# Fetching the first token half's columns a block earlier, splitting block 7's sums, and ordering W2's splits last

## The chip, the cores and the metric

The kernel runs on one core of one Trainium2 chip. The metric is the device time of one execution in microseconds (us), as the median of several runs. TensorE is called PE here, VectorE DVE, ScalarE ACT, GpSimd POOL and SyncE SP. "L669" is line 669 of the kernel before.

## What is computed

One layer of a streaming encoder over 1024 tokens of 1024 channels, all in float32: a mixer (a convolution group and a retention group between one input and one output projection), then a feed-forward part, then a last norm.

```python
x = x + jnp.concatenate([a_out, b_out], axis=-1) @ w_out[l]
h = rms_norm(x, norm2_g[l])
x = x + jnp.square(jax.nn.relu(h @ w_ff1[l])) @ w_ff2[l]     # 1024 x 4096, 4096 x 1024
...
return rms_norm(x, final_g)
```

The change lies in the passage from the output projection to the feed-forward part, and at the seam between the feed-forward's two products.

## The kernel before

**Tiles.** Tokens are cut into 8 blocks of 128. Every float32 matmul is done as three matmuls of rounded halves (`mm3`, L137, with its lines 139 to 141): each operand is split into a high part, which ACT writes, and a low part, which DVE makes by subtraction. `split_evac` (L189, with lines 190 and 191) does this for a tile of 128 partitions.

**The feed-forward part as a 2 x 2 scheme with seven products.** W1's columns go in 16 pairs of 128-column blocks, tokens in two halves of 512 (blocks 0 to 3 and 4 to 7), channels in two halves. `strassen_pair` (L747) computes a pair with seven products of 512 columns, M1 to M7, each 4 steps of `mm3`, so 12 matmuls. M1 and M2 take the first token half's columns (B11, B21) and a plain W1 block. The other five need sums: of W1 blocks (`prep_sums`, L702, DVE lines 679 to 682, then splits), and of columns: T2 for M6, T1 for M5, T3 for M7, B22 for M3, T4 for M4. `prep_sums` loads two W1 blocks (L687) into a pool `rawp` of two buffers.

**Where the columns come from.** A block's output projection adds to the residual (L815). `normed_columns` (L619) then norms the block (L622), transposes it on PE (L632), and writes its columns. A block of the first half is split to B11 and B21, and a full copy goes to DRAM (L641, then L617 on ACT's queue). A block of the second half reads back the partner block's copies (L649 and L650, on SP's queue, 256 KB each in runs of 512 bytes), copies b12 (L652) and makes four sums (L653, L654, L657, L658) with their splits. T3 and T4 of blocks 4 to 6 go to DRAM (L617 on POOL's queue) and come back as one load each (L830, 768 KB, the "early" columns) to be split at L838; block 7's T3 and T4 are split at once.

**Order of the work.** The blocks run as ORDER = 0, 1, 4, 2, 5, 3, 6, 7, normed one block behind their projection. Four pairs (AHEAD = 4) are started before the second half is complete: a pair that runs ahead is a generator with stops after its first load and split, and after M1 and M2. The sequence behind the loop over blocks (L825 to L838): M1 and M2 of pair 0; new T3 and T4 tiles; the early columns' loads; block 7's columns and sums; M1 and M2 of pair 1; pairs 2 and 3; the splits of the early columns. Then each pair is run to its end, pair 0 first.

**What sets the order on an engine.** A list scheduler places instructions on each engine by the order in which they are written and by when it reckons their inputs ready. On the chip each engine and each queue then runs its list strictly in that order, waiting where an input is missing. Tiles come from pools with a fixed number of slots: `sp` has 11 of 2 KB per partition (sums, copies, fetched columns, hidden rows), `wp` 13 of 8 KB (columns and W2), `ps` and `pr` four PSUM banks each.

**The seam.** The second product (`ff2_group`, L864) loads W2 (L877) into `wp` slots that the last pair's column tiles give up, and the kept sums of the hidden rows (xr, L893); `split_unit` (L859) splits both. Its first product M1 adds into four banks of `ps`; one of these is the last pair's `pa`, read last by ACT rl (L728) and DVE hid (L723). `copy` (L758, ACT line 760) copies a product out of PSUM; PE may not add to that bank before.

Of the kernel before, what the change touches and what calls it, by code (L numbers as in the profile page):

```python
# [15 lines left out]
P = 128  # L16
# [25 lines left out]
def hybrid_layer_kernel(  # L42
# [89 lines left out]
    def load_split(src, scales):  # L132
        return split(load_raw(src), scales)

    pe_log, tap_log = [], []

    def mm3(acc, lh, ll, rh, rl, first, last, loose=False):  # L137
        kw = dict(skip_group_check=True) if loose else {}
# [47 lines left out]
                nc.tensor.transpose(out=pt[:, i], in_=src[:, d * P : (d + 1) * P], identity=ident)  # L186
            split_evac(pt, dst.quad(g, 0, t), dst.quad(g, 1, t))

    def split_evac(src, hi, lo):  # L189
        nc.scalar.activation(hi, src, AF.Copy)  # L190
        nc.vector.tensor_tensor(lo, src, hi.bitcast(F32), ALU.subtract)  # L191


# [421 lines left out]
    def keep_columns(name, cols, t):  # L615
        eng = nc.scalar if name in ("B11", "B21") else nc.gpsimd
        eng.dma_start(dram_cols[name][:, :, cols], t)  # L617

    def normed_columns(b, r):  # L619

        xn = cp.tile([P, D], F32, tag="c", name="xn")
        nc.vector.scalar_tensor_tensor(xn, flat(b), r, n2row, ALU.mult, ALU.mult)  # L622
        j, t = divmod(b, 4)
        cols = slice(t * P, (t + 1) * P)
        hl = lambda name: [h[:, :, cols] for h in hb[name]]
        new = lambda name: sp.tile([P, 4, P], F32, tag="s", name=name)
        pts = []
        for k in range(2):
            pt = pr.tile([P, 4, P], F32, tag="r", name="pt")
            for i in range(4):  # L630
                d = 4 * k + i
                nc.tensor.transpose(out=pt[:, i], in_=xn[:, d * P : (d + 1) * P], identity=ident)  # L632
            pts.append(pt)
        if j == 0:
            if t == 0:
                new_columns("B11")
                new_columns("B21")
            for name, pt in zip(("B11", "B21"), pts):
                split_evac(pt, *hl(name))
                full = new("full")  # L640
                nc.scalar.activation(full, pt, AF.Copy)  # L641
                keep_columns(name, cols, full)
            return
        if t == 0:
            new_columns("T2", True)
            new_columns("T1")
            new_columns("B22")
        b11, b21 = new("b11"), new("b21")
        nc.sync.dma_start(b11, dram_cols["B11"][:, :, cols])  # L649
        nc.sync.dma_start(b21, dram_cols["B21"][:, :, cols])  # L650
        b12, t2 = new("b12"), new("t2")
        nc.scalar.activation(b12, pts[0], AF.Copy)  # L652
        nc.vector.tensor_tensor(b11, b12, b11, ALU.subtract)  # L653
        nc.vector.tensor_tensor(t2, pts[1], b11, ALU.subtract)  # L654
        split_evac(t2, *hl("T2"))
        split_evac(b11, *hl("T1"))
        nc.vector.tensor_tensor(b12, pts[1], b12, ALU.subtract)  # L657
        nc.vector.tensor_tensor(b21, b21, t2, ALU.subtract)  # L658
        split_evac(pts[1], *hl("B22"))
        for name, full in (("T3", b12), ("T4", b21)):  # L660
            if b < NB - 1:
                keep_columns(name, cols, full)
            else:
                split_evac(full, *hl(name))

# [79 lines left out]
    def strassen_pair(p, ahead):  # L747

        a, b = {}, hb

        def product(acc, name, first, last):
            for d in range(4):
                mm3(
                    acc, a[name][0][:, d], a[name][1][:, d], b[name][0][:, d], b[name][1][:, d],
                    first and d == 0, last and d == 3, loose=True,
                )

        def copy(acc):  # L758
            t = sp.tile([P, HALF], F32, tag="s", name="part")
            nc.scalar.activation(t, acc, AF.Copy)  # L760
            return t

        def plus(acc, t):
            nc.vector.tensor_tensor(t, acc, t, ALU.add)
            return t

        raw = [load_w1(2 * p + i) for i in range(1 if ahead else 2)]
        split_named(a, raw[0], ("M1", "M2"))
        if ahead:
            yield  # L770
        if not ahead:
            prep_sums(a, raw)
        pa = ps.tile([P, HALF], F32, tag="mm", name="pa")
        product(pa, "M1", True, False)
        m1 = copy(pa)
        pb = pr.tile([P, HALF], F32, tag="r", name="pb")
        product(pb, "M2", True, True)
        c11 = square(plus(pb, m1))
        if p < NPAIR - 1:
            keep(p, "M1", c11)  # L780
        if ahead:
            yield
            prep_sums(a, [load_w1(2 * p + i) for i in range(2)])
            c11 = sp.tile([P, HALF], F32, tag="s", name="hid")
            nc.sync.dma_start(c11, xs[p]["M1"])
        product(pa, "M6", False, False)
        u2 = copy(pa)
        pb = pr.tile([P, HALF], F32, tag="r", name="pb")
        product(pb, "M5", True, False)
        m5 = copy(pb)  # L790
        product(pa, "M7", False, False)
        c22 = square(plus(pa, m5))
        product(pb, "M3", False, True)
        c12 = square(plus(pb, u2))
        product(pa, "M4", False, True)
        c21 = square(pa, relu(pa))
        if p < NPAIR - 1:
            keep_operands(p, c11, c12, c21, c22)
        else:
            for i, row in enumerate(((c11, c12), (c21, c22))):  # L800
                for j, t in enumerate(row):
                    nc.gpsimd.dma_start(last_hid[i][:, j * HALF : (j + 1) * HALF], t)
# [6 lines left out]
    for i, b in enumerate(ORDER):  # L809
        if i + 3 < NB:  # L810
            conv_norm(ORDER[i + 3])
        if i + 2 < NB:
            conv_side(ORDER[i + 2])
        for n, acc in enumerate(out_proj(woa, *sides.pop(b))):
            nc.vector.tensor_tensor(blk[b][:, n], acc, blk[b][:, n], ALU.add)  # L815
        m = tiny.tile([P, 1], F32, tag="nmr", name="m2")
        nc.gpsimd.tensor_tensor(m, mean_sq(flat(b)), eps1, ALU.add)
        rn[b] = tiny.tile([P, 1], F32, tag="r1", name="rn")
        nc.gpsimd.tensor_tensor(rn[b], m, mhalf[:, 0:1], ALU.pow)
        if i >= 6:  # L820
            next(pairs[i - 6])
        if i >= 1:
            normed_columns(ORDER[i - 1], rn.pop(ORDER[i - 1]))
    hb["M1"], hb["M2"] = hb["B11"], hb["B21"]
    next(pairs[0])  # L825
    for name in ("T3", "T4"):
        new_columns(name)
    early = slice(0, HALF - P)
    for name in ("T3", "T4"):
        nc.sync.dma_start(hb[name][1][:, :, early].bitcast(F32), dram_cols[name][:, :, early])  # L830
    normed_columns(NB - 1, rn.pop(NB - 1))
    next(pairs[1])
    for p in range(2, AHEAD):
        next(pairs[p])
        next(pairs[p])
    for name in ("T3", "T4"):
        hi, lo = (t[:, :, early] for t in hb[name])
        split_evac(lo.bitcast(F32), hi, lo)  # L838
    for product, name in (("M3", "B22"), ("M4", "T4"), ("M5", "T1"), ("M6", "T2"), ("M7", "T3")):
# [18 lines left out]

    def split_unit(src, n):  # L859
        w = wp.tile([P, 2, n, HALF], F32R, tag="w", name="w")  # L860
        split_evac(src, w[:, 0], w[:, 1])
        return w

    def ff2_group(group):  # L864
# [174 lines left out]
```

## Time and profile before

| | us |
|---|---|
| median of 3 runs | 1062.36 (1060.86 to 1062.65) |
| the profiled execution | 1062.97 |
| its span, first to last instruction | 1061.2 |
| PE busy in it | 1030.1 (97%) |
| DVE busy | 804.8 (76%) |
| ACT busy | 377.0 (36%) |
| POOL busy | 129.4 (12%) |

The profile is that of one execution; its times are counted from the first instruction. PE is busy for nearly all of the span, so its few idle stretches are looked at one by one: the timeline of an engine shows each instruction's start and length and, in brackets, the idle time before it and what ended that. A start on a queue (SPq, ACTq) is that of a transfer's issue; it lands later. The granted clock is the share of full speed that the throttle gives PE: 1.00 is 2.4 GHz, 0.50 is 1.2 GHz.

### The profile page before, as it was taken

The numbers are of one execution on the slowest core, as the hardware profiler recorded it, in microseconds if no ns is written. First come the engines' busy times: TensorE is split into PE (matmuls) and PEld (weight loads), VectorE is DVE, ScalarE is ACT, GpSimd is POOL, SyncE is SP. The second block draws the span as 40 slices with busy tenths as digits, with TensorE's granted clock in tenths as the row PEclk, the third lists the DMA queues.
The fourth block names the chain that finished last, engine by engine and source line by source line (L and its number), as shares of the span: only waits on it lengthen the run. The fifth ranks groups of instructions, "written<-read, shape, count | busy, mean of one in ns | idle before, by whom it ended". The sixth has DMA issues, their size and how long they took to land.

```text
span 1061.2 us, 12636 instructions
## 1 busy us (share of the span) xinstructions
PE 1030.1 (97%) x4744; PEld 854.5 (81%) x4744; DVE 804.8 (76%) x998; ACT 377.0 (36%) x600; POOL 129.4 (12%) x241
## 2 busy tenths in 40 slices
PE   9999999999999999699999999999999999999996
PEld 8788888888888878477888888887888888888885
DVE  6297769998797468757776777766988778777757
ACT  7511111144520567323332332222543433333323
POOL 0400110022000122012121211211000000000003
PEclk9999999999999999799999999999999999999998
DMA  9712011102152024545443344437464354252224
GB/s 362 153 56 80 20 60 60 40 1 80 42 177 80 1 78 151 187 141 197 160 179 141 147 160 139 179 139 295 141 215 162 100 184 173 100 186 92 96 73 158
DMA packets 51197, 137.52 MB, mean 130 GB/s; under 512 B 6656, under 2 KB 16000, under 8 KB 51136
## 3 DMA queue, kind: packets, MB, share of 16 engines
q1 hardware_dynamic: 37712, 104.46, 29.8%
q0 software_dynamic: 9200, 30.15, 7.3%
q10 hardware_dynamic: 4224, 2.10, 0.7%
q8 instruction: 37, 0.61, 0.2%
q14 instruction: 24, 0.20, 0.1%
HBM read 100.25 MB, written 36.44 MB: 129 GB/s over the span
## 4 chain that ended last, share of the span: by engine, by line
PE 80%; DVE 8%; DMA 5%; issue 3%; ACT 2%; POOL 1%; SPq 1%; POOLq 0%; DVEq 0%; ACTq 0%
PE acc L139 18%; PE acc L140 18%; PE acc L141 18%; PE pa L139 5%; PE pa L141 5%; PE pa L140 5%; PE pb L139 3%; PE pb L140 3%; PE pb L141 3%; DVE y L383 2%; DMA raw<-in_w_in_dram 2%; DMA raw<-in_w_dram 1%; DMA w2raw<-in_w_dram 1%; DMA b<-colsB 1%; DVE hid L723 1%
## 5 line engine op out<-in xcount | busy, mean ns | idle before, releaser
L139 PE MATMUL acc<-w 128*128 128x512 f32 x454 | 176.7, 389 | 0.1
L140 PE MATMUL acc<-w 128*128 128x512 f32 x454 | 176.2, 388 | 0.0
L141 PE MATMUL acc<-w 128*128 128x512 f32 x454 | 176.1, 388 | 0.0
L383 DVE SCALAR_TENSOR_TENSOR y<-glu,vec,y 128x1024 f32<-128x1024 f32 x120 | 153.7, 1289 | 2.0
L139 PEld LDWEIGHTS acc<-w 128*128 128x128 f32 x454 | 85.2, 188 | 19.2 <-issue 0.7
L139 PE MATMUL acc<-w,cols 128*128 128x512 f32 x256 | 100.0, 391 | 0.0
L140 PE MATMUL acc<-w,cols 128*128 128x512 f32 x256 | 99.8, 390 | 0.0
L141 PE MATMUL acc<-w,cols 128*128 128x512 f32 x256 | 99.8, 390 | 0.0
L141 PEld LDWEIGHTS acc<-w 128*128 128x128 f32 x454 | 85.2, 188 | 17.7
L140 PEld LDWEIGHTS acc<-w 128*128 128x128 f32 x454 | 85.2, 188 | 17.3
L190 ACT ACTIVATE w<-xr 128x1024 fp32r<-128x1024 f32 (+1 forms) x56 | 56.3, 1005 | 104.6 <-PE acc L141 66.9
L139 PE MATMUL pa<-h,w1h 128*128 128x512 f32 x192 | 76.4, 400 | 12.3 <-ACT w1h L190 10.0
L191 DVE TENSOR_TENSOR w<-xr,w 128x1024 fp32r<-128x1024 f32 (+1 forms) x56 | 64.6, 1154 | 28.2 <-ACT w L190 26.9
L908 DVE TENSOR_TENSOR blk<-acc,blk 128x512 f32<-128x512 f32 x112 | 72.4, 684 | 11.0 <-PE acc L141 11.0
L141 PE MATMUL pa<-h,w1l 128*128 128x512 f32 x192 | 76.6, 399 | 2.2 <-DVE w1l L191 2.2
L139 PE MATMUL pb<-h,w1h 128*128 128x512 f32 x192 | 75.2, 392 | 0.0
L140 PE MATMUL pb<-h,w1h 128*128 128x512 f32 x192 | 74.7, 389 | 0.0
L141 PE MATMUL pb<-h,w1l 128*128 128x512 f32 x192 | 74.7, 389 | 0.0
L116 ACT ACTIVATE w<-raw 128x1024 fp32r<-128x1024 f32 (+1 forms) x36 | 34.8, 966 | 97.3 <-PE acc L141 70.3
L190 ACT ACTIVATE w1h<-t 128x1024 fp32r<-128x1024 f32 x32 | 33.8, 1059 | 70.2 <-PE pb L141 40.6
L141 PEld LDWEIGHTS acc<-w,cols 128*128 128x128 f32 x256 | 48.1, 188 | 9.9
L139 PEld LDWEIGHTS acc<-w,cols 128*128 128x128 f32 x256 | 48.1, 188 | 9.9
(189 smaller groups left out, 2012.7 us busy)
## 6 DMA issues: line engine op xcount, KB each, us to landing
raw<-in_w_dram SPq DMA_DIRECT2D x38, 512.0 KB, 3.6
w2raw<-in_w_dram SPq DMA_DIRECT2D x30, 512.0 KB, 4.5
raw<-in_w_in_dram SPq DMA_DIRECT2D x23, 512.0 KB, 3.3
xt<-in_x_dram SPq DMA_DIRECT2D x8, 512.0 KB, 8.1
raw<-in_w_out_dram SPq DMA_DIRECT2D x8, 512.0 KB, 3.3
xr<-in_x_dram SPq DMA_DIRECT2D x16, 256.0 KB, 3.0
out_dram<-ot SPq DMA_DIRECT2D x16, 256.0 KB, 2.0
xcol<-in_x_cols_dram SPq DMA_DIRECT2D x7, 512.0 KB, 6.8
```

Source lines behind the costliest of these rows:

```text
L116: nc.scalar.activation(w[:, 0, i], raw[:, i], AF.Copy)
L139: nc.tensor.matmul(acc, lhsT=lh, rhs=rh, start=first, stop=False, **kw)
L140: nc.tensor.matmul(acc, lhsT=lh, rhs=rl, start=False, stop=False, **kw)
L141: pe_log.append(nc.tensor.matmul(acc, lhsT=ll, rhs=rh, start=False, stop=last, **kw))
L190: nc.scalar.activation(hi, src, AF.Copy)
L191: nc.vector.tensor_tensor(lo, src, hi.bitcast(F32), ALU.subtract)
L383: nc.vector.scalar_tensor_tensor(y, glu[c][:, k : k + S], tap(k), y, ALU.mult, ALU.add)
L723: nc.vector.scalar_tensor_tensor(t, src, 0.0, rl, ALU.max, ALU.mult)
L908: nc.vector.tensor_tensor(t, acc[lane][r], t, ALU.add)
```

## The change

`fetch_columns` reads the partner block's copies before the block in front is normed, one block earlier than before. `normed_columns` of a second-half block now stops after T2 and T1 and returns the remaining five DVE steps as a function, `rest`; for blocks 4 to 6 it is called at once, for block 7 only after pair 0's weight sums. Pair 0 gets one more stop, after `prep_sums`. Block 7's columns come directly behind pair 0's M1 and M2, and the early columns' loads and splits move behind pair 3's M1 and M2. `copy` notes its ACT instruction; `split_unit` places each of its ACT splits behind the last one noted, which is pair 15's second copy (m5).

```diff
--- before.py
+++ after.py
@@ -132,7 +132,17 @@
     def load_split(src, scales):
         return split(load_raw(src), scales)
 
-    pe_log, tap_log = [], []
+    pe_log, tap_log, act_log = [], [], []
+
+    def hold(ins, until):
+
+        name = lambda i: i.ins if hasattr(i, "ins") else i
+        tc.add_manual_dep(
+            name(ins),
+            name(until).name,
+            mybir.DependencyInfo(mybir.DependencyClass.NoSync, mybir.DependencyReason.DATA),
+            reason="others first",
+        )
 
     def mm3(acc, lh, ll, rh, rl, first, last, loose=False):
         kw = dict(skip_group_check=True) if loose else {}
@@ -186,8 +196,10 @@
                 nc.tensor.transpose(out=pt[:, i], in_=src[:, d * P : (d + 1) * P], identity=ident)
             split_evac(pt, dst.quad(g, 0, t), dst.quad(g, 1, t))
 
-    def split_evac(src, hi, lo):
-        nc.scalar.activation(hi, src, AF.Copy)
+    def split_evac(src, hi, lo, after=None):
+        act = nc.scalar.activation(hi, src, AF.Copy)
+        if after is not None:
+            hold(act, after)
         nc.vector.tensor_tensor(lo, src, hi.bitcast(F32), ALU.subtract)
 
 
@@ -615,6 +627,14 @@
     def keep_columns(name, cols, t):
         eng = nc.scalar if name in ("B11", "B21") else nc.gpsimd
         eng.dma_start(dram_cols[name][:, :, cols], t)
+
+    fetched = {}
+
+    def fetch_columns(b):
+
+        fetched[b] = [sp.tile([P, 4, P], F32, tag="s", name=name.lower()) for name in ("B11", "B21")]
+        for t, name in zip(fetched[b], ("B11", "B21")):
+            nc.sync.dma_start(t, dram_cols[name][:, :, (b - 4) * P : (b - 3) * P])
 
     def normed_columns(b, r):
 
@@ -640,28 +660,30 @@
                 full = new("full")
                 nc.scalar.activation(full, pt, AF.Copy)
                 keep_columns(name, cols, full)
-            return
+            return None
         if t == 0:
             new_columns("T2", True)
             new_columns("T1")
             new_columns("B22")
-        b11, b21 = new("b11"), new("b21")
-        nc.sync.dma_start(b11, dram_cols["B11"][:, :, cols])
-        nc.sync.dma_start(b21, dram_cols["B21"][:, :, cols])
+        b11, b21 = fetched.pop(b)
         b12, t2 = new("b12"), new("t2")
         nc.scalar.activation(b12, pts[0], AF.Copy)
         nc.vector.tensor_tensor(b11, b12, b11, ALU.subtract)
         nc.vector.tensor_tensor(t2, pts[1], b11, ALU.subtract)
         split_evac(t2, *hl("T2"))
         split_evac(b11, *hl("T1"))
-        nc.vector.tensor_tensor(b12, pts[1], b12, ALU.subtract)
-        nc.vector.tensor_tensor(b21, b21, t2, ALU.subtract)
-        split_evac(pts[1], *hl("B22"))
-        for name, full in (("T3", b12), ("T4", b21)):
-            if b < NB - 1:
-                keep_columns(name, cols, full)
-            else:
-                split_evac(full, *hl(name))
+
+        def rest():
+            nc.vector.tensor_tensor(b12, pts[1], b12, ALU.subtract)
+            nc.vector.tensor_tensor(b21, b21, t2, ALU.subtract)
+            split_evac(pts[1], *hl("B22"))
+            for name, full in (("T3", b12), ("T4", b21)):
+                if b < NB - 1:
+                    keep_columns(name, cols, full)
+                else:
+                    split_evac(full, *hl(name))
+
+        return rest
 
 
 
@@ -757,7 +779,7 @@
 
         def copy(acc):
             t = sp.tile([P, HALF], F32, tag="s", name="part")
-            nc.scalar.activation(t, acc, AF.Copy)
+            act_log.append(nc.scalar.activation(t, acc, AF.Copy))
             return t
 
         def plus(acc, t):
@@ -783,6 +805,8 @@
             prep_sums(a, [load_w1(2 * p + i) for i in range(2)])
             c11 = sp.tile([P, HALF], F32, tag="s", name="hid")
             nc.sync.dma_start(c11, xs[p]["M1"])
+            if p == 0:
+                yield
         product(pa, "M6", False, False)
         u2 = copy(pa)
         pb = pr.tile([P, HALF], F32, tag="r", name="pb")
@@ -819,21 +843,27 @@
         nc.gpsimd.tensor_tensor(rn[b], m, mhalf[:, 0:1], ALU.pow)
         if i >= 6:
             next(pairs[i - 6])
+        if b >= 4:
+            fetch_columns(b)
         if i >= 1:
-            normed_columns(ORDER[i - 1], rn.pop(ORDER[i - 1]))
+            rest = normed_columns(ORDER[i - 1], rn.pop(ORDER[i - 1]))
+            if rest:
+                rest()
     hb["M1"], hb["M2"] = hb["B11"], hb["B21"]
     next(pairs[0])
     for name in ("T3", "T4"):
         new_columns(name)
+    rest = normed_columns(NB - 1, rn.pop(NB - 1))
+    next(pairs[1])
+    for p in range(2, AHEAD):
+        next(pairs[p])
+    next(pairs[2])
+    next(pairs[0])
+    rest()
+    next(pairs[3])
     early = slice(0, HALF - P)
     for name in ("T3", "T4"):
         nc.sync.dma_start(hb[name][1][:, :, early].bitcast(F32), dram_cols[name][:, :, early])
-    normed_columns(NB - 1, rn.pop(NB - 1))
-    next(pairs[1])
-    for p in range(2, AHEAD):
-        next(pairs[p])
-        next(pairs[p])
-    for name in ("T3", "T4"):
         hi, lo = (t[:, :, early] for t in hb[name])
         split_evac(lo.bitcast(F32), hi, lo)
     for product, name in (("M3", "B22"), ("M4", "T4"), ("M5", "T1"), ("M6", "T2"), ("M7", "T3")):
@@ -858,7 +888,7 @@
 
     def split_unit(src, n):
         w = wp.tile([P, 2, n, HALF], F32R, tag="w", name="w")
-        split_evac(src, w[:, 0], w[:, 1])
+        split_evac(src, w[:, 0], w[:, 1], act_log[-1] if act_log else None)
         return w
 
     def ff2_group(group):
```

## Rows read from the trace of the kernel before

**Rows 1.** Waits of PE, whole span: us in total, times, longest

```profile
PE pa L139 <- ACT w1h L190: 10.0, 1, 10.0
...
PE pt L564 <- ACT a L567: 1.2, 2, 0.7
```

**Rows 2.** PE timeline, 420 to 456: start, us, instruction, [idle before]

```profile
421.95 1.03 PE L632 MATMUL pt<-ident,xn 128*128 128x128 f32 x8
...
437.74 0.39 PE L141 MATMUL pb<-h,w1l 128*128 128x512 f32 x1
448.15 0.79 PE L139 MATMUL pa<-h,w1h 128*128 128x512 f32 x1 [10.02 <-ACT w1h L190]
...
453.85 0.40 PE L140 MATMUL pb<-h,w1h 128*128 128x512 f32 x1
```

**Rows 3.** Windows, PE alone: busy time, granted clock, DMA share, GB/s

```profile
452.00:453.00 1.00, 1.00 (x3) 0.50 0.95 268
```

**Rows 4.** Chain that ended last, in order of time: start, us, what

```profile
427.13 7.47 DMA b<-colsB
...
727.95 10.11 DMA w2raw<-in_w_dram
...
745.24 0.50 PE acc L139
```

**Rows 5.** SP timeline, issues, 424 to 449

```profile
424.65 2.36 SPq L830 DMA_DIRECT2D h<-colsT  x2
...
428.50 20.07 SPq L687 DMA_DIRECT2D raw<-in_w_dram  x3
```

**Rows 6.** DVE timeline, 430 to 452

```profile
430.83 1.76 DVE L191 TENSOR_TENSOR h<-h,h 128x1536 fp32r<-128x1536 f32 x1 [3.23 <-ACT h L190]
434.69 0.69 DVE L653 TENSOR_TENSOR b<-b,b 128x512 f32<-128x512 f32 x1 [2.10 <-DMA b<-colsB]
...
446.33 0.68 DVE L680 TENSOR_TENSOR t<-t,raw 128x512 f32<-128x512 f32 x1
...
449.88 1.22 DVE L191 TENSOR_TENSOR w1l<-t,w1h 128x1024 fp32r<-128x1024 f32 x1
```

**Rows 7.** ACT timeline, the last write of block 3's columns

```profile
415.39 0.52 ACTq L617 DMA_DIRECT2D colsB<-full  x1
```

**Rows 8.** Landing times: column writes L617; fetches (tile b); pair 0's first load

```profile
DMA to landing us min/median/max: 2.4/2.5/5.2
...
DMA to landing us min/median/max: 2.5/2.9/7.6
...
DMA to landing us min/median/max: 9.6/9.6/9.6
```

**Rows 9.** PE timeline at the seam of the two products, 729 to 745

```profile
729.88 0.39 PE L141 MATMUL pb<-h,w1l 128*128 128x512 f32 x1
732.58 0.50 PE L139 MATMUL pa<-h,w1h 128*128 128x512 f32 x1 [2.32 <-ACT part L760]
...
737.26 0.39 PE L140 MATMUL pb<-h,w1h 128*128 128x512 f32 x1
...
742.50 0.39 PE L139 MATMUL acc<-w 128*128 128x512 f32 x1
...
744.76 0.39 PE L140 MATMUL acc<-w 128*128 128x512 f32 x1
```

**Rows 10.** ACT timeline at the seam, then one row of DVE's

```profile
730.99 1.06 ACT L190 ACTIVATE w<-w2raw 128x1024 fp32r<-128x1024 f32 x1 [8.25 <-DMA w2raw<-in_w_dram]
...
741.88 1.07 ACT L190 ACTIVATE w<-xr 128x1024 fp32r<-128x1024 f32 x1 [2.68 <-DMA xr<-x1M]
742.84 0.58 ACT L728 ACTIVATE rl<-pa 128x512 f32<-128x512 f32 x1
...
744.50 0.68 DVE L723 SCALAR_TENSOR_TENSOR hid<-pa,rl 128x512 f32<-128x512 f32 x1
```

**Rows 11.** Waits of SP, 370 to 460: us in total, times, longest

```profile
SPq L649 <- PE acc L141: 10.8, 2, 8.2
```

## The prediction

> **What bounds the kernel now.** The table of shares comes first: TensorE (PE) is busy for 1030.1 of 1061.2 us, so 31.1 us at most can be won without taking matmuls away, and this change takes none away. Next, the list of what PE waited for [rows 1]: one wait of 10.0 us, for a split of W1 sums on ScalarE (ACT), stands out; PE's timeline gives it its full price, and shows a second one at the seam of the feed-forward's two products. At a steady pitch a matmul starts every 0.226 us (742.50 to 744.76 is ten steps, [rows 9]).
>
> Stall A [rows 2]: after the matmul at 437.74 the next was due at 437.97 and came at 448.15: 10.18 us. Then 13 matmuls, from 448.15 to 453.85, take 5.70 us where 13 x 0.226 = 2.94 would do: 2.76 more. In 452 to 453 the granted clock is still 0.50 of full, the lower level (1.2 of 2.4 GHz) [rows 3]; the matmul at 453.85 has its full speed back. Stall A costs 12.9 us.
>
> Stall B [rows 9]: due at 730.11, came at 732.58, 2.47 us; from there to 737.26, 13 matmuls in 4.68 us, 1.74 too many. Together 4.2 us.
>
> Last, the chain of work that ended last [rows 4], because it says which stall sets the end. It goes through the transfer b<-colsB (427.13, 7.47 us), which is what leads to A. It does **not** go through B: there it follows the transfer w2raw (727.95, 10.11 us), steps of VectorE (DVE), and PE at 745.24. A is on the path; B lies beside it.
>
> **Part 1, the fetch.** SP issues its transfers in order. It issues L830 at 424.65 [rows 5], then block 7's fetch from 427.13 [rows 4], and then from 428.50 the two loads of pair 0's W1 blocks [rows 5]. Block 7's first sum L653 starts at 434.69, when its fetch has landed; DVE sat idle for 3.23 us before 430.83 and for 2.10 us before 434.69, and pair 0's sums, up to L680 at 446.33, queue behind [rows 6]. In the new order block 7's fetch stands ahead of L830. It reads block 3's columns, whose last write is issued at 415.39 [rows 7] and lands 2.5 us later (median), at 417.9; a fetch takes 2.9 us (median), to 420.8 [rows 8]. Block 7's transposes end at about 423.0 (421.95 + 1.03, [rows 2]), so its fetch is then no longer late. The wait of 2.10 us goes, and four of its sums and splits (4 x 0.60 = 2.4 us at DVE's pitch) move into the time in which DVE stood still.
>
> **Part 2, the split of block 7.** Pair 0's weight sums are traced ahead of block 7's last five DVE steps, of pair 3's products and of the early columns' splits. So what is late next are pair 0's two loads. The first is issued at 428.50 and lands 9.6 us later [rows 8], at 438.1. From 424.65 on SP had 2 x 768 KB (L830), 2 x 256 KB (fetch) and 2 x 512 KB in flight: 3072 KB in 13.4 us. Without the fetches, 2560 KB at the same rate take 11.2 us, to 435.8: an estimate. Its ends: 433.5, if SP, which the fetches no longer hold, also issues both loads about 2.3 us earlier, and 438.1, if nothing is won. From landing to PE it takes L679 (0.60) and then what lay between L680 at 446.33 and PE at 448.15, 1.82 [rows 2, 6]: 2.4 us. PE could start at 438.2; due is 437.97. Ends 435.9 and 440.5: no wait at all, or 2.5 us and the loss at the lower clock that followed the 2.47 us of B, 1.74: 4.2.
>
> Behind this stands DVE's own load: from 434.69 to 451.1 (449.88 + 1.22) it ran almost without a gap, 16.4 us [rows 6]. Of it 2.4 now come earlier, and pair 1's sum and square (1.2) as well; 12.8 us from 435.8 end at 448.6. PE needs, a product every 12 x 0.226 = 2.71 us, M6 at 437.97, M5 440.7, M7 443.4, M3 446.1 and M4 448.8. That can just be met, with M7 the tightest: it needs T3, whose last step ends after the sums (2.4), two splits (2.4), one of 0.6 and the five steps (3.0), 8.4 us after 435.8 or 444.2, unless they fill the earlier gaps. I charge **1.0 us** for M6 and M7, nearer to none (the estimates miss by 0.2 and 0.8); ends 0 and 4.2.
>
> Moved with it: the early columns' loads and splits follow pair 3 in the trace. At 430.83 the first of these splits filled an idle stretch of DVE [rows 6], and can do so again. The later pairs get their weight buffers when pair 0's steps free them, so they move along with PE; I charge nothing, within the ends above.
>
> **The fetches of blocks 4 to 6.** The fetched tiles are held one block longer, out of eleven slots for which SP already waits: L649 waited 10.8 us for PE in two waits, up to 8.2 [rows 11]. PE's own idle time there was 1.2 us, behind ACT a [rows 1]. So 1.2 us are won at best, and at worst a block waits the 8.2. I take 0, because PE hardly idled there although the slots were already short.
>
> **Part 3, W2's splits last.** ACT held w<-w2raw at 730.99, behind its transfer, ahead of the copy that PE waited for [rows 9, 10]. With the hold that copy runs when M6 ends, about 727.5, and the 4.2 us of B go. But the second product's fourth accumulator needs the bank of pair 15, which comes free after ACT rl (742.84) and DVE hid (744.50) [rows 10]. rl stands on ACT behind w<-xr, which waits for its transfer until 741.88; hid stands on DVE behind steps that begin when w2raw has landed, 738.06 [rows 4]. The edit moves none of these. PE would do its 11 matmuls from 738.3 instead of from 742.50 [rows 9], stand idle from 740.8, and resume at the same 745.24 [rows 4]. Ends: -1.1 us, if hid runs straight behind rl (742.84 + 0.58 + 0.68 = 744.1), and +2.76, if the new idle time of 4.4 us lowers the clock as A did. I take the middle, **+0.8**.
>
> [...]
>
> **Sum.** -12.9 + 1.0 + 0 + 0.8 = -11.1 us. The profiled execution took 1062.97 us around its span of 1061.2, so 1051.9 by it. It lies 0.6 above the median of the three runs (1062.36), from which I forecast **1051.3 us**.
>
> **Rivals.**
> 1. *B pays too.* ACT takes rl ahead of w<-xr, and DVE hid at once: -4.2 replaces +0.8, 1046.3. For it: the hold changes ACT's order there. Against: the chain goes through w2raw, and rl already stood behind w<-xr. Chance 0.13.
> 2. *The loads or T3 are late.* PE waits at M6 or at M7 up to the end above, 4.2 in place of 1.0: 1054.5; at both, 1058.7. For it: the loads took 9.6 us in company, and M7 has no slack. Chance 0.22. The Trainium skill, page "DMA: Bandwidth & Descriptors", section "Issuing engines are not separate DMA queues", says that all transfers, whoever issues them, interleave on the same 16 DMA engines. The 9.6 us of the loads agree. By that rule an earlier fetch doesn't hasten loads that still share with L830, and this rival's 1054.5 would hold.
> 3. *Slower: the slots.* Tiles held a block longer make columns or convolution tiles wait for a slot, and PE's transposes with them. From 11.1 us of new PE idle time on, the gain is gone; two blocks that lose the longest slot wait, 8.2 us each, give 1051.3 + 16.4 = 1067.7. For it: SP's waits. Against: PE idled only 1.2 us there. Chance 0.10.
> 4. *The fetch goes out no earlier,* because no slot is free: A stays, about 1062.4. Against: SP issued block 7's fetch right behind L830, not behind a slot. Chance 0.06.
>
> **How the numbers follow.** Forecast (1049 to 1053.5) 0.49, rival 1 0.13, rival 2 0.22, rival 3 0.10, rival 4 0.06. The range leaves out rivals 3 and 4 (0.16) and the far edges of 1 and 2: 1046.0 to 1057.5. A measurement of this kernel can tell about 0.2% (2.1 us) from no change. Faster by more: 0.49 + 0.13 + 0.22 = 0.84; within it 0.05, most of rival 4; slower 0.11, rival 3 and the rest.
>
> **What would show it.** Right: block 7's fetch ahead of L830 on SP and landed before 425; L653 near 424; no PE gap over 2.5 us between 430 and 450 and no lower clock there; at the seam a PE gap of about 4 us inside the second product's first matmuls, behind DVE hid. Wrong: the split of pair 0's sums still more than 3 us behind pair 3's products, PE gaps of over 3 us between 370 and 414, or rl ahead of w<-xr and no gap at the seam.

## The result and the profile after

| us | before | after |
|---|---|---|
| median (4 runs each) | 1062.51 (1060.86 to 1065.08) | 1052.29 (1048.85 to 1052.68) |
| ratio, 95% interval | | 0.9895 [0.9866, 0.9923] |
| the profiled execution, its span | 1062.97, 1061.2 | 1052.13, 1050.4 |
| PE busy in it | 1030.1 | 1027.5 |

The change makes the kernel faster, by 10.2 us in the medians; 1051.3 was forecast. Two of its terms were wrong, though, in opposite directions, so that the nearness is partly luck, and one of the three edits turned out not to be needed.

First the list of waits of PE in the kernel after, from 425 to 745 us (us in total, times, longest). It answers to [rows 1] and to the waits of [rows 9].

```profile
PE pa L151 <- DVE w1l L203: 2.7, 3, 1.2
PE acc L149 <- DVE hid L745: 1.7, 1, 1.7
PE pa L149 <- ACT w1h L200: 1.0, 2, 0.7
PE pb L149 <- ACT part L782: 0.5, 1, 0.5
PE pa L150 <- DVE h L203: 0.3, 1, 0.3
PE pa L149 <- DVE part L786: 0.2, 1, 0.2
```

The wait of 10.0 us is gone, and so is the one of 2.3 us for an ACT copy at the seam. In their place stand nine short ones of 6.4 us together; the kernel before had three, of 3.2 us, beside the two long ones. PE's timeline shows where (start, us, instruction, [idle before]):

```profile
438.52 0.39 PE L149 MATMUL pa<-h,w1h 128*128 128x512 f32 x1
...
439.42 0.50 PE L151 MATMUL pa<-h,w1l 128*128 128x512 f32 x1 [0.29 <-DVE w1l L203]
445.39 0.50 PE L149 MATMUL pb<-h,w1h 128*128 128x512 f32 x1 [0.46 <-ACT part L782]
446.43 0.50 PE L150 MATMUL pa<-h,w1h 128*128 128x512 f32 x1 [0.31 <-DVE h L203]
451.77 0.47 PE L149 MATMUL pa<-h,a 128*128 128x512 f32 x1 [0.24 <-DVE part L786]
468.75 0.50 PE L149 MATMUL pa<-h,w1h 128*128 128x512 f32 x1 [0.39 <-ACT w1h L200]
471.14 0.50 PE L151 MATMUL pa<-h,w1l 128*128 128x512 f32 x1 [1.19 <-DVE w1l L203]
484.78 0.50 PE L149 MATMUL pa<-h,w1h 128*128 128x512 f32 x1 [0.66 <-ACT w1h L200]
487.18 0.80 PE L151 MATMUL pa<-h,w1l 128*128 128x512 f32 x1 [1.19 <-DVE w1l L203]
...
490.64 0.40 PE L150 MATMUL pa<-tx,w1h 128*128 128x512 f32 x1
```

Where stall A stood [rows 2], M6 of pair 0 now starts at 438.52 with no idle time before it. Four waits remain inside pair 0, two each in pairs 2 and 3. The chain that ended last now goes through two loads of W1 blocks (5.57 us at 460.06, 5.68 us at 475.98) and, as before [rows 4], through w2raw, which for its part is now followed by hid and PE.

To compare executions, times are counted here from the start of the first block's transposes (370.57 before, 371.23 after), because executions differ by up to about 2 us ahead of it. The table says how many us earlier than in the kernel before each point is reached. M6 of a pair is its second matmul, "seam" the tenth matmul of the second product, "end" PE's last matmul of all. In the kernels without the hold (before, e2, e3, e4, e10) PE waits for hid two matmuls later, so there that wait shows only in "end". e1 to e10 are the kernels of the next section.

| | M6 pair 0 | M6 pair 1 | M6 pair 3 | M6 pair 15 | seam | end |
|---|---|---|---|---|---|---|
| after | 10.65 | 10.58 | 10.29 | 8.82 | 11.22 | 11.50 |
| e0, the same kernel again | 10.65 | 11.41 | 10.69 | 9.15 | 10.86 | 11.11 |
| e1, hold alone | 0.44 | 1.10 | 1.12 | -0.43 | 1.59 | 1.82 |
| e2, after without hold | 10.69 | 11.21 | 11.52 | 11.54 | 13.80 | 10.29 |
| e3, early fetch alone | 4.78 | 4.51 | 4.70 | 4.74 | 6.91 | 5.00 |
| e4, after without fetch and hold | 10.52 | 12.17 | 11.84 | 11.91 | 13.67 | 12.08 |
| e6, after without fetch | 10.48 | 10.78 | 9.40 | 10.14 | 12.34 | 10.94 |
| e5, second unit's splits behind rl | 10.65 | 12.25 | 11.62 | 11.68 | 13.85 | 14.10 |
| e7, weight sums ahead of xsum | 10.65 | 11.46 | 14.27 | 15.93 | 18.13 | 16.77 |
| e7b, the same kernel again | 10.68 | 11.90 | 14.71 | 16.37 | 20.02 | 20.26 |
| e9, e7 with two orders at the seam | 10.66 | 12.00 | 14.81 | 16.47 | 20.69 | 21.06 |
| e10, e7 without hold | 10.71 | 11.72 | 14.53 | 16.17 | 18.10 | 16.55 |

The end of the output projection is missing from it: it stays within 0.04 us of the kernel before in all of them.

### The profile page after: what moved, and what is told of

It is laid out like the page before. It is cut to its first block, busy times and chain, and to the rows that moved or that the text cites. A ratio compares the mean times of both kernels' runs of the same rounds, so it can differ in the third digit from the quotient of the medians.

```text
span 1050.4 us, 12634 instructions
## 1 busy us (share of the span) xinstructions
PE 1027.5 (98%) x4744; PEld 852.5 (81%) x4744; DVE 804.2 (77%) x998; ACT 377.7 (36%) x600; POOL 129.4 (12%) x241
## 4 chain that ended last, share of the span: by engine, by line
PE 79%; DVE 7%; issue 5%; DMA 4%; ACT 2%; POOL 2%; SPq 1%; POOLq 0%; DVEq 0%; ACTq 0%
PE acc L149 18%; PE acc L150 18%; PE acc L151 18%; PE pa L151 4%; PE pa L149 4%; PE pa L150 4%; PE pb L151 3%; PE pb L150 3%; PE pb L149 3%; DVE y L395 2%; DMA raw<-in_w_in_dram 2%; DMA raw<-in_w_dram 1%; DMA w2raw<-in_w_dram 1%; DVE cols L253 1%; DVE w L117 1%
```

## The experiments

Kernels that ran side by side (e1 to e4; e0, e5, e6 and e7; e7b, e9 and e10) share the runs of the kernel before. Ratios are against it, with 95% intervals.

**e1: the hold alone.** The kernel before with part 3 only: W2's ACT splits stand behind m5, which is the last of pair 15's three copies (m1, u2, m5).

```diff
...
-        split_evac(src, w[:, 0], w[:, 1])
+        split_evac(src, w[:, 0], w[:, 1], act_log[-1] if act_log else None)
```

> Part 3 alone: the kernel before with only the hold on W2's splits. Theory 1 (that of the prediction: the chain through w2raw and w<-xr ends last whatever ACT does) expects no gain, 0 to +2.8 us against the kernel before, first accumulation after the wait for DVE hid no earlier than before counted from pair 15's M7 (15.1 us). Theory 2 (read from the trace after the change: the hold also reorders SP and DVE there, the xr load goes ahead of the second half of w2raw and two ysum steps behind hid) expects -2.4 to -3 us, that distance 12.0 us.

Measured: 1060.69 us, 0.9988 [0.9974, 1.0002]. The median is 0.9 us lower than that of the kernel before, which the interval does not tell from nothing. In the trace the seam gains 2.25 us (-0.43 at M6 of pair 15, 1.82 at the end). The price that the prediction set on it, +0.8, does not appear.

**e2: all but the hold.**

```diff
-        split_evac(src, w[:, 0], w[:, 1], act_log[-1] if act_log else None)
+        split_evac(src, w[:, 0], w[:, 1])
```

> Parts 1 and 2 without part 3: the changed kernel with the hold taken off. Theory 1 expects about 1051.5, 0.8 better than the changed kernel. Theory 2 expects 2.4 to 3 us worse than the changed kernel, 1054.5 to 1055.5, with the 2.3 us PE wait for ACT part back and the lower clock behind it.

Measured: 1051.12 us, 0.9893 [0.9867, 0.992]; not to be told from the changed kernel. Its trace says more: from M6 of pair 15 to the end e2 loses 1.25 us (11.54 to 10.29), while the changed kernel gains 2.65 (8.82 to 11.47 at the second product's 41st matmul). That difference of 3.9 us is not seen in the medians, and some 1.5 us of it are a low clock behind e2's wait for hid (732.8 to 736.3). The next section shows what stands against it in pair 3.

**e3: the early fetch alone.** The kernel before with `fetch_columns` called a block ahead.

```diff
...
-        b11, b21 = new("b11"), new("b21")
-        nc.sync.dma_start(b11, dram_cols["B11"][:, :, cols])
-        nc.sync.dma_start(b21, dram_cols["B21"][:, :, cols])
+        b11, b21 = fetched.pop(b)
...
+        if b >= 4:
+            fetch_columns(b)
```

> Part 1 alone: the kernel before with the fetches a block earlier; order of block 7, pair 0 and early columns as before, no hold. If the fetch behind SP's wait is what makes stall A (theory 1), the wait of DVE at L653 goes, pair 0's loads land near 436, and M6 of pair 0 starts at 439 to 442 instead of 448.15: -7 to -10 us. If it is DVE's queue ahead of pair 0's sums that makes A (rival), the sums stay behind all of block 7, M6 starts at 444 or later, and less than 5 us are won.

Measured: 1057.79 us, 0.9959 [0.9944, 0.9973]. By the trace it wins 4.8 us at M6 of pair 0, and half of stall A stays. SP's, DVE's and PE's timelines in e3:

```profile
428.42 1.49 SPq L693 DMA_DIRECT2D raw<-in_w_dram  x2
...
435.87 1.75 DVE L191 TENSOR_TENSOR h<-h,h 128x1536 fp32r<-128x1536 f32 x1
...
441.61 0.68 DVE L685 TENSOR_TENSOR t<-raw 128x512 f32<-128x512 f32 x1
...
444.64 0.80 PE L139 MATMUL pa<-h,w1h 128*128 128x512 f32 x1 [5.32 <-ACT w1h L190]
```

The loads of pair 0 land 7.5 to 8.2 us after their issue, so both had landed by 438.1 (428.42 + 1.49 + 8.2). The first sum, L685, starts at least 3.5 us after that, at 441.61, and no idle time stands before it: from 432.86 on DVE ran without a gap through block 7's last splits, the splits of the early columns (435.87, 1.75 us) and the products' sums. So once the fetch is early, DVE's order, and not a transfer, holds PE for 3.5 of its 5.3 us or more.

**e4 and e6: all but the early fetch,** without the hold (e4) and with it (e6). The fetch is called inside `normed_columns`, where its loads stood before; everything else is written as in the changed kernel.

```diff
             new_columns("B22")
+        fetch_columns(b)
         b11, b21 = fetched.pop(b)
...
-        if b >= 4:
-            fetch_columns(b)
```

> Part 2 alone: block 7's sums in two parts around pair 0's weight sums and early columns behind pair 3, but each fetch where the block is normed, as before; no hold. Theory 1: block 7's fetch no longer stands behind the early columns' loads on SP, since these now follow in the trace, so most of the gain comes from here too: M6 starts before 442, -6 to -9 us. Rival (the early fetch is needed): L653 still waits until after 432 and M6 starts after 444, less than 5 us won.

> Parts 2 and 3 without part 1: the changed kernel with each fetch where its block is normed. Theory A (after the runs of single parts: the order around pair 0's sums is what matters, the early fetch adds nothing to it) expects the changed kernel's time within 1.5 us. Theory B (the prediction's: the early fetch takes the DVE wait at L653 away) expects 2 us or more over it.

Measured: e4 1051.82 us, 0.9901 [0.9877, 0.9925]; e6 1048.93 us, 0.9864 [0.9845, 0.9882], beside e0, the changed kernel run again next to e6, at 1050.01 us, 0.9867 [0.9848, 0.9887].

> The changed kernel once more, beside the variants below on the same chip. Measures what they are compared with, and whether the low-clock stretch at 487 us (pair 3, after waits of 0.66 and 1.19 us) belongs to the program or to the execution. If to the program: M6 of pair 4 again starts 8.8 us earlier than before against the transposes' start; if to the execution: up to 11.5 us, as in the run without the hold.

e0's question has no plain answer in its own trace: M6 of pair 4 comes 9.15 us earlier, near the 8.8 that would speak for the program, with the granted clock at 0.50 from 486.4 to 489.9. The next section sets it beside e2 and e5.

The edit that fetches early adds nothing to the rest of the change. SP's issues in e6 show why:

```profile
417.08 1.56 SPq L637 DMA_DIRECT2D b<-colsB  x2
426.09 2.04 SPq L710 DMA_DIRECT2D raw<-in_w_dram  x2
```

and in the changed kernel:

```profile
417.33 0.52 SPq L637 DMA_DIRECT2D b<-colsB  x1
418.61 0.52 SPq L637 DMA_DIRECT2D b<-colsB  x1
426.63 2.68 SPq L709 DMA_DIRECT2D raw<-in_w_dram  x2
429.48 0.53 SPq L866 DMA_DIRECT2D h<-colsT  x1
```

Block 7's fetch leaves at 417 to 419 in both. Once the 768 KB loads of the early columns are written behind pair 3 instead of ahead of block 7, nothing stands in front of the fetch on SP, and the list scheduler places it that early by itself. So the fetch is early in all of these kernels, and what the rest of the change would be worth with a late one, no run here shows.

**e5: the second W2 unit's ACT splits behind rl.** In the changed kernel PE still waits 1.7 us at the seam for hid. This edit lets ACT rl go ahead of the splits that stood before it.

```diff
...
-        nc.scalar.activation(rl, acc, AF.Relu)
+        rl_log.append(nc.scalar.activation(rl, acc, AF.Relu))
...
-        split_evac(src, w[:, 0], w[:, 1], act_log[-1] if act_log else None)
+        splits.append(n)
+        split_evac(src, w[:, 0], w[:, 1], act_log[-1] if len(splits) < 3 else rl_log[-1])
```

> The changed kernel, with the splits of W2's second unit held behind ACT rl of the last pair, so that rl no longer stands behind the split of xr. Theory: PE's wait for DVE hid (1.67 us at 733.97) goes, as rl and hid then follow pair 15's M4 at once, and the seam gains 1.2 to 1.7 us more: 1050.5 to 1051 where the changed kernel stands at 1052.3. Rival: PE then waits for the second unit's splits, which come 1 us later, and nothing is won.

Measured: 1050.03 us, 0.9866 [0.9848, 0.9884], the time of e0 (1050.01). PE waits 1.9 us for hid, as it did. ACT did what was asked; DVE's timeline in e5 shows why it was not enough:

```profile
727.59 0.60 ACT L750 ACTIVATE rl<-pa 128x512 f32<-128x512 f32 x1 [5.43 <-PE pa L151]
...
728.48 1.23 DVE L913 TENSOR_TENSOR ysum<-w2raw 128x1024 f32<-128x1024 f32 x1 [2.17 <-DMA w2raw<-in_w_dram]
729.62 1.22 DVE L918 TENSOR_TENSOR ysum<-w2raw 128x1024 f32<-128x1024 f32 x1
730.75 0.68 DVE L745 SCALAR_TENSOR_TENSOR hid<-pa,rl 128x512 f32<-128x512 f32 x1
```

rl is done at 728.2, and hid could follow. On DVE, though, it stands behind two W2 differences, the first of which waits for w2raw to land. The theory that ACT's order alone makes the wait fell.

**e7: the waits of pairs 2 and 3.** Theory: pair 2's sums are late because their load is late, and the load is late because the buffer it needs is given back by DVE's split a<-raw, which stood behind four steps xsum of the pair in front. The edit traces a pair's weight sums ahead of the xsum steps of the pair in front, for pairs 1 to 3.

```diff
-            if p == 0:
-                yield
+            yield
...
         c21 = square(pa, relu(pa))
+        if ahead:
+            yield
...
+    for p in range(AHEAD):
+        next(pairs[p])
+        if p + 1 < AHEAD:
+            next(pairs[p + 1])
+        for _ in pairs[p]:
+            pass
```

> The changed kernel, with the weight sums of pairs 1 to 3 traced ahead of the hidden rows' sums (xsum) of the pair before; on DVE only the split of a22 moves, 2.4 us ahead. Theory: this split frees the buffer of the next pair's second W1 block, whose load (5.6 us) then lands 2.4 us earlier, and the waits of PE for w1h and w1l in pairs 2 and 3 (0.39, 1.19, 0.66 and 1.19 us) and the low clock behind them go: M6 of pair 4 starts 1.5 to 3 us earlier than in the changed kernel. Rival: PE then waits in these pairs for the xsum steps' slots or for the loads all the same, and nothing moves.

Measured: 1046.41 us, 0.9828 [0.9809, 0.9848], 3.6 us below e0, which ran beside it. DVE in the changed kernel (first fence) and in e7 (second):

```profile
456.81 0.68 DVE L701 TENSOR_TENSOR xsum<-hid 128x512 f32<-128x512 f32 x1
...
459.34 0.69 DVE L203 TENSOR_TENSOR a<-raw,a 128x512 fp32r<-128x512 f32 x1
...
465.65 0.69 DVE L701 TENSOR_TENSOR t<-raw 128x512 f32<-128x512 f32 x1 [1.94 <-DMA raw<-in_w_dram]
```

```profile
455.75 0.69 DVE L203 TENSOR_TENSOR a<-raw,a 128x512 fp32r<-128x512 f32 x1
...
460.78 0.69 DVE L701 TENSOR_TENSOR t<-raw 128x512 f32<-128x512 f32 x1 [1.81 <-DMA raw<-in_w_dram]
```

The split moved up past four steps of 0.6 us, the load went out at 456.46 instead of 460.06, and pair 2's first sum starts 4.9 us earlier. PE's waits in pairs 2 and 3 are gone. The theory holds, and the gain is larger than the 1.5 to 3 us expected: M6 of pair 15 comes 7.1 us earlier than in the changed kernel, and 4.3 earlier than in e5, which lost nothing to the clock there. The split is the first link, not the only step that moved: DVE's sums behind it and one ACT split changed places too, so the 3.6 us belong to the edit as a whole.

**e7b, e9, e10: the same once more, then with the seam mended, then without the hold.** e9 is e7's kernel with e5's hold behind rl and, on DVE, the second unit's first difference behind hid:

```diff
...
-                    nc.vector.tensor_tensor(sums[i], y(0, 1), y(0, 0), ALU.subtract)
+                    dif = nc.vector.tensor_tensor(sums[i], y(0, 1), y(0, 0), ALU.subtract)
+                    if i == 1:
+                        hold(dif, hid_log[-1])
```

> The kernel of e7 once more, to stand beside the next two. If its lead over the changed kernel is real and not the luck of its runs, its median stands again 3 to 4 us below the 1050.0 of the changed kernel's repeat (1046 to 1047 with the kernel before at 1062 to 1064), PE's list of waits has no w1l and no w1h row, and the wait for DVE hid at the seam is again about 1.9 us. Rival: the lead was chance, and the median is within 1 us of 1050.

> e7 with, at the seam, two more orders: the second W2 unit's ACT splits behind ACT rl, and its first DVE difference (L912 in the changed kernel) behind DVE hid, both of pair 15. Theory: PE's last wait, 1.87 us for hid, came from what stood ahead on both engines: in e7 ACT made w<-w2raw and w<-xr (724.24 to 726.2) before rl, although pair 15's last matmul ended at about 723.6; with rl alone moved (e5) DVE's differences behind the landing of w2raw (728.48, 729.62) kept hid as late as before. With both moved rl starts at about 723.8, hid ends near 725.1, and PE's tenth matmul waits for nothing. The second unit's splits start some 0.6 to 1.3 us later and are wanted 5 us later. Expected: no hid row in PE's list of waits, end 1.9 us earlier, median 1044 to 1045. Rival: the second unit's splits become the next wait (PE waits 1 to 2 us for w at the 25th matmul), and the median stays within 0.7 us of e7's.

> e7 without the hold on W2's splits (part 3 of the change). Theory from the traces: the hold is worth 2.3 to 3.9 us at the seam, so the median is 2 to 4 us above e7's (1048 to 1050), and in the trace hid stands behind three differences of the second unit on DVE and PE waits 3 us or more for ACT parts and hid at the seam, with a low clock after. Rival: the medians of the runs so far (0.9 us for the hold alone on the kernel before, nothing that can be told apart on the changed one) are the truth, and the median is within 1 us of e7's.

Measured side by side: e7b 1044.33 us, 0.9833 [0.9815, 0.9851]; e9 1041.68 us, 0.981 [0.9794, 0.9827]; e10 1046.08 us, 0.9846 [0.9831, 0.986].

e7's lead repeats. e9 is the fastest here and beats both kernels, by 20.3 us the kernel before. Its list of waits of PE from 425 to 745 has one row left, the copy's 0.5 us that the changed kernel has too. Above that row e7 has the first of these fences, and e10 the second (both also wait 0.3 us for DVE h):

```profile
PE acc L149 <- DVE hid L745: 1.9, 1, 1.9
```

```profile
PE pa L149 <- ACT part L782: 2.0, 1, 2.0
PE acc L149 <- DVE hid L745: 1.6, 1, 1.6
```

In e9 hid runs straight behind rl and ahead of the difference:

```profile
721.44 0.60 ACT L750 ACTIVATE rl<-pa 128x512 f32<-128x512 f32 x1 [5.60 <-PE pa L151]
...
722.07 0.69 DVE L745 SCALAR_TENSOR_TENSOR hid<-pa,rl 128x512 f32<-128x512 f32 x1 [1.93 <-ACT rl L750]
722.67 1.22 DVE L920 TENSOR_TENSOR ysum<-w2raw 128x1024 f32<-128x1024 f32 x1
```

Both engines' orders together made the wait; DVE's order alone was not changed in any run. How much it costs depends on when w2raw lands: in e7 the wait is 1.87 us with a low clock behind it, in e7b, the same kernel, 0.4 us. So e9's lead over e7b is 2.6 us in the medians but 0.8 in the two traces (21.06 against 20.26 us at the end), and their intervals overlap.

e10's order is as expected: ACT's copy waits again behind w<-w2raw for 2.0 us, and hid stands behind three W2 differences, at 728.40. Its median is 1.75 us above e7b's, short of the 2 to 4 expected, and the two intervals overlap. No low clock followed its waits, which the expectation had counted in.

## Why the prediction was right, and where it was wrong

**Stall A: right.** 10.18 us and the 2.76 of low clock behind it were to go; the changed kernel has no wait ahead of M6 of pair 0, a granted clock of 1.00 in the windows from 440 to 460, and reaches that M6 10.65 us earlier.

**Part 1: the wait went, but the edit was not needed.** The prediction let the early fetch take DVE's wait of 2.10 us at L653 away, and named L653 (after: L671) near 424 as its sign. The fetch did land early and the wait is gone, but the step runs at 427.08, behind a product's sum, a weight split and a square on DVE (hid at 426.48). The edit itself brought nothing: e4 and e6 have A's gain without it, because the fetch leaves as early there, and e3, with the fetch alone, has 4.8 us of it. What removes the rest of A is the order of the writing: weight sums ahead of block 7's last steps and of the early columns' splits on DVE, and the early columns' loads behind the W1 loads on SP; these two were not run apart. The W1 loads now land 3.4 to 5.5 us after their issue, not 9.6 [rows 8]; in e3, where only the fetches are gone from ahead of them, it is 7.5 to 8.2. The first sum starts at 434.53, as the second load lands, against an estimate of 435.8 for the landing. The prediction's bound of 433.5 to 438.1 held. It treated the fetch's place on SP and the loads' place as two effects; the second brought the first with it.

**The residual, +1.0: mis-sized in this execution.** A's 12.9 us have become 8.82 at M6 of pair 4, and stay so to pair 15: 4.1 lost, not 1.0. Counted from the start of one matmul to the next against the steady 0.226 us, as the prediction counts A, the rows say where. Pair 0's four waits cost 2.4 us: M6 0.6 and M7 0.6, together close to the 1.0 charged for them, and M3 0.7 and M4 0.5, which wait for a copy and a sum out of PSUM and for which nothing was charged. The four waits of pairs 2 and 3 cost 4.4, where the kernel before lost 4.2 in pairs 1 to 3, so "they move along with PE; I charge nothing" was right to 0.2 us. A low clock behind the last of them costs 1.65 (487.18 above: 8 steps to 490.64 take 3.46 us, where 8 x 0.226 = 1.81 would do). Together 2.4 + 0.2 + 1.65 = 4.2. So the term left out M3 and M4 of pair 0 and a clock that fell behind a wait of 1.19 us, as it had not behind the same wait in the kernel before.

The low clock is the largest of these, and it belongs to the execution, not to the program. PE's timeline of e2, whose instructions stand in the same order on every engine and queue up to the seam, at the step that stands at 487.18 in the changed kernel:

```profile
484.49 0.50 PE L151 MATMUL pa<-h,w1l 128*128 128x512 f32 x1 [1.18 <-DVE w1l L203]
...
486.43 0.39 PE L150 MATMUL pa<-tx,w1h 128*128 128x512 f32 x1
```

The wait is the same; eight steps take 3.46 us in the changed kernel and 1.94 in e2. A window of 1 us of the changed kernel shows the lower of the two levels, 1.2 GHz (length, PE busy, granted clock, DMA share, GB/s); in e2 the windows from 484 to 488 have 1.00:

```profile
488.00:489.00 1.00, 1.00 (x3) 0.50 0.13 49
```

e0 and e5 have that order up to the seam as well. Their windows around the same wait (length, busy time of PE, its weight loads, DVE, ACT and POOL, granted clock, DMA share, GB/s), e0 first:

```profile
480.00:490.00 10.00, 8.10 (x27) 5.92 (x27) 9.19 (x14) 4.09 (x5) 2.05 (x4) 0.83 0.32 100
480.00:490.00 10.00, 8.18 (x36) 6.12 (x35) 9.47 (x14) 4.67 (x6) 2.27 (x5) 1.00 0.35 116
```

So of four executions with one order two lost the clock here. Where it held, the residual was near the forecast: 1.4 in e2, 1.3 in e5, and 1.0 in e4, whose order differs a little; it was 3.8 in e0, and 2.8 in e6, whose clock fell in pair 2. In the profiles, then, what e2 loses at its seam it had not lost in pair 3. That this is why its median equals that of the changed kernel is not shown, since one execution of each was traced.

**The fetches of blocks 4 to 6, 0: right.** The output projection ends within 0.04 us of the kernel before in every run; rival 3 is dead, and so is rival 4, as block 7's fetch went out at 417.33. SP's fetches still wait, up to 7.9 us for a slot that DVE's tx gives back and longer for the copies to be written, but PE's waits from 370 to 420 are the same two, 1.2 and 0.2 us.

**Part 3, +0.8: wrong in sign.** This is the step that failed. The stretch from M6 of pair 15 on gained 2.65 us. B's 4.2 went, as forecast, and PE was to stand 4.4 us for the fourth accumulator, since the edit "moves none of these": neither w<-xr behind its transfer nor hid behind the W2 differences [rows 10]. It moved both. ACT, DVE, SP and PE at the seam of the changed kernel:

```profile
730.70 1.06 ACT L200 ACTIVATE w<-w2raw 128x1024 fp32r<-128x1024 f32 x1 [6.07 <-DMA w2raw<-in_w_dram]
731.67 1.04 ACT L200 ACTIVATE w<-xr 128x1024 fp32r<-128x1024 f32 x1
732.61 0.57 ACT L750 ACTIVATE rl<-pa 128x512 f32<-128x512 f32 x1
```

```profile
730.70 1.22 DVE L912 TENSOR_TENSOR ysum<-w2raw 128x1024 f32<-128x1024 f32 x1 [1.70 <-DMA w2raw<-in_w_dram]
...
733.22 0.69 DVE L745 SCALAR_TENSOR_TENSOR hid<-pa,rl 128x512 f32<-128x512 f32 x1 [0.16 <-ACT rl L750]
```

```profile
713.75 1.89 SPq L907 DMA_DIRECT2D w2raw<-in_w_dram  x4
715.74 0.48 SPq L923 DMA_DIRECT2D xr<-x1M  x1
719.41 3.30 SPq L907 DMA_DIRECT2D w2raw<-in_w_dram  x4
```

```profile
733.97 0.50 PE L149 MATMUL acc<-w 128*128 128x512 f32 x1 [1.67 <-DVE hid L745]
```

And in the kernel before, SP's issues and the last step on DVE ahead of hid (744.50 in [rows 10]):

```profile
721.91 8.96 SPq L877 DMA_DIRECT2D w2raw<-in_w_dram  x8
730.97 0.38 SPq L893 DMA_DIRECT2D xr<-x1M  x1
...
743.37 1.21 DVE L887 TENSOR_TENSOR ysum<-w2raw 128x1024 f32<-128x1024 f32 x1
```

Before, SP issued xr<-x1M at 730.97, behind all eight loads of w2raw; now it goes at 715.74, between the fours, so w<-xr follows w<-w2raw without a wait [rows 10 have 2.68]. And hid no longer stands behind the two later differences (L887 before, L917 after). The hold constrains only ACT splits, but the list scheduler plans all engines and queues from the same list: with the splits later it found other places for the xr load and for hid. e1, with the hold alone, shows the same order on SP (xr at 723.51 between two fours) and on DVE. The wait for hid remains, 1.67 us, because rl still waits for w2raw's landing on ACT.

Rival 1 had the right mechanism (hid earlier) at too large a price: it gave back all 4.2. Its bet was that ACT takes rl ahead of w<-xr; ACT did not, w<-xr merely stopped waiting.

What the hold is worth: 0.9 us in the medians for e1, 1.75 for e10 against e7b, each within its intervals, and nothing for e2, whose ratio equals the changed kernel's. The traces are clearer. From M6 of pair 15 to the end, every one with the hold gains more than every one without. With it: 2.68 (after), 1.96 (e0), 2.25 (e1), 0.80 (e6), 0.84 (e7) and 3.89 (e7b). Without: 0 (before), -1.25 (e2), 0.26 (e3), 0.17 (e4) and 0.38 (e10). In e6, e7, before and e2 a low clock stands behind a wait there. Among the rest of the kernels without e7's edit it is 1.96 to 2.68 against 0.17 and 0.26, so some 2 us. The sign is thus shown by the traces; the size moves with low-clock stretches that cost some 1.5 us each and come and go between executions.

The Trainium skill, page "TensorE: Matmul & The Clock Gate", section "HAM oscillation — how this bites in real kernels", tells of a kernel whose matmuls ran cold behind every wait for data, waits longer than the short ones here. The traces agree in part: behind the 1.67 us of the changed kernel the clock stays at 1.00 in the windows from 730 to 750, behind the 1.87 us of e7 it falls.

**The sum.** -12.9 + 4.1 + 0 - 2.65 = -11.5 us instead of -11.1; 0.66 us more ahead of the first transposes make the span's -10.8. The forecast of 1051.3 is only 1.0 off the median of 1052.29, because a residual 3.1 us too small and a seam 3.5 us too dear nearly cancelled. That is luck. In e5, whose seam gained 2.42 us and whose clock held, the end comes 14.1 us earlier, not 11.1.

## What to carry to other kernels

When a stall is removed, follow every product behind it and the next users of the same buffers too, not only the next two products: here the load of pair 2 hung on a split that stood behind four unrelated steps, and the edit that moved it was worth 3.6 us in the medians. A hold on one engine's instructions can re-plan the others in a list scheduler (here SP's and DVE's order, not POOL's); read the new order of all engines, and do not price them as unmoved. And before crediting a part of a change, test whether the rest of it brings the same effect along: the edit for the early fetch was given a part of the gain in the forecast, and on the chip the rest of the change fetched as early without it.

## What the runs showed of the hardware that was not expected

The same wait of the same instruction list is followed by a lower clock in one execution and not in the next. Behind 1.18 to 1.20 us at pair 3 the granted clock is 0.50 in the changed kernel and e0, and 1.00 in e2 and e5, all four with one order up to there; behind pair 2's 1.19 us it stays at 1.00 in the changed kernel, and in e6, behind 1.20 us at 470.84, it is 0.50:

```profile
471.00:472.00 1.00, 1.00 (x3) 0.50 0.69 270
```

The idle time just ahead does not tell the two apart: the clock fell in e1 behind 0.32 and 1.19 us at pair 3, and held in e0 behind 0.77 and 1.20 us at pair 2.

At the seam e7 and e7b, one kernel, differ by 3.5 us at the end (16.77 and 20.26 us earlier than before): 0.4 of it are there at M6 of pair 15 already, 1.5 come from the wait, 1.87 against 0.4 us, as w2raw lands at another time, and 1.5 from the clock, since in e7 eleven steps behind the wait take 4.21 us (727.50 to 731.71), in e7b 2.67. Such a wait is thus a lottery of some 1.5 us in each execution. That would fit the spread of the changed kernel, 1048.4 to 1052.7 us over its two sets of runs, though only two of these were traced; one trace is not enough to price such a wait.
